# A decoder layer with Strassen-like products: sixteen modulations of single token tiles on VectorE instead of ScalarE, and one store of FF1 on ScalarE's queue

## The chip, the cores and the metric

One core of a Trainium2 chip. It has five engines that each work through a list of their own: TensorE (PE, with its weight loads as PEld), VectorE (DVE), ScalarE (ACT), GpSimd (POOL) and SyncE (SP), and 16 DMA engines that several queues share. The queues are named for the engine that issues to them: in the table of queues of the profile q1 is SP's, q10 is ACT's and q0 is POOL's. The time is the device time of one execution in microseconds, as the median of several runs of the same program.

## The reference

One layer of a decoder trunk, 1024 tokens by 1024 channels, in float32. The part around the change:

```python
x  = layer_norm(ALPHA * x + (1.0 + gt1) * mixed, ln1_g, ln1_b)
u2 = x * (1.0 + sc2) + sh2
h  = square(relu(u2 @ w_ff1 + b_ff1))              # 1024 -> 4096
x  = layer_norm(ALPHA * x + (1.0 + gt2) * (h @ w_ff2 + b_ff2), ln2_g, ln2_b)
```

`mixed` comes from attention and a gated delta rule, whose work lies before the change. `sc2` and `sh2` have one value for each channel; the kernel folds the gain and shift of the first norm into them.

## The kernel before

All large products are made from two-part numbers: a float32 tile is split into a high part (ACT copies it into the rounded format, line 215) and a low part (DVE subtracts, line 216), and each product takes three matmuls: high by high, low by high, high by low. Names that end in `h` and `l`, or `wh` and `wl`, are such parts. A matmul of 128x512 takes 0.23 us from start to start.

FF1 and FF2 are further made with seven products in place of eight, so sums and differences of blocks are needed of the tokens, of the weights and of h. The 1024 tokens are eight tiles of 128, and `TILE = [[0, 2, 4, 5], [1, 3, 6, 7]]` puts them into two halves. A pair of tiles, one of each half, has one number j.

**Order.** PE, DVE and ACT run in program order: `at(p, f)` puts a function at position p, `after(n, f)` n positions from now, and `run_events` calls what is due ahead of each matmul. A position is one 128x512 matmul. What an engine is given by an earlier event stands ahead of what a later one gives it, whether its inputs are there or not. The DMAs issued on SP and POOL are ordered by the scheduler, and those on ACT stand in ACT's own list.

**From the mix to FF1.** The stage that ends the mix has four segments of 96 matmuls. As its token tiles are ended, `mix_done` normalises them (lines 1356 to 1368). Then `u2_turn(j, us, ks)` transposes a tile on PE, four blocks of 128x128 to one PSUM bank (line 1379, tile `b`, two banks in turn), and `put` writes each block with scale and shift into `rawu` (line 1382): position 2 + i after the transposes for block i. Tiles 0 to 3 are turned in pairs, two blocks of either half at a time (`n` = 2). Tiles 4 to 7 come one at a time (`n` = 1): two calls for each, of four blocks. Tiles 6 and 7 are turned after FF1 has begun. `rawu` is then split by `quad_split` into `u11`, `u21` and `u22`, and after the sums of `t_sums` and `t_one` by `t_split` into `mh` and `ml`, which FF1 reads from its fifth product on (the matmul that writes `c` from `mh`).

**FF1.** Sixteen pairs of blocks of `w_ff1`, seven products of 12 matmuls each (line 1841). `w_go` and `w_split` split the weights of the next pair, `f_sums` and `f_sums2` (DVE, lines 1407 and 1516) make their sums in `fraw`. Biases, relu and squares are on ACT (lines 1558 to 1578). The block results `t` (six buffers) are stored to `hf_d` (line 1554) in pieces c0, c2 and c3 by ACT's queue, and the sums: `h_sums` (line 1585 on) makes S1 in `a21` and S2, S3 in `sa`, which go out by SP's queue, as `h_sums2` does with `sb`. `again` (line 1581) reads c0 back for the first five pairs.

**FF2.** It reads `hf_d` and weights in 56 chunks `sraw` of two tiles (lines 1706 and 1712), splits them to `sp` and multiplies (line 1901). The first two chunks are loaded on ACT's queue while FF1 still runs, the rest by SP.

Of the kernel before, what the change touches and what calls it, by code (L numbers as in the profile page):

```python
# [12 lines left out]
AF = mybir.ActivationFunctionType  # L13
ALU = mybir.AluOpType
# [3 lines left out]
P = 128  # L18
# [16 lines left out]
def hybrid_layer_kernel(ctx: ExitStack, tc: tile.TileContext,  # L35
                        x, c, w_ada, b_ada, w_in, conv_w, a_log, dt_bias, sinks, dn_norm_w,
                        w_oa, w_ob, w_out, ln1_g, ln1_b, w_ff1, b_ff1, w_ff2, b_ff2,
                        ln2_g, ln2_b, out, dbg=None):
    nc = tc.nc
    x, c, out = x[0], c[0], out[0]  # L40
# [6 lines left out]
    V, A, G, T = nc.vector, nc.scalar, nc.gpsimd, nc.tensor  # L47
# [7 lines left out]
    def psum(tag, bufs, name=None):  # L55
        return ps.tile([P, HALF], F32, tag=tag, bufs=bufs, name=name or tag)
# [140 lines left out]
    def at(p, f, *args):  # L197
        order[0] += 1
        heapq.heappush(events, (p, order[0], f, args))

    def after(n, f, *args):
        at(count[0] + n, f, *args)
# [62 lines left out]
    sh2 = const.tile([P, KT], F32, name="sh2")  # L265
    sc2 = const.tile([P, KT], F32, name="sc2")
# [182 lines left out]
    for step in steps.split():  # L449
        f, k = step[0], int(step[1])  # L450
# [50 lines left out]
    with tc.tile_pool(name="pa", bufs=2, side="right") as pa:  # L501
        if True:
# [43 lines left out]
            for m in (13, 11, 9, 7, 5, 3, 1):  # L546
# [5 lines left out]
                                   op0=ALU.mult, op1=ALU.mult)  # L552
# [69 lines left out]
        for h in range(8):  # L622
# [7 lines left out]
            for half in range(2):  # L630
                tp = psum("c", 1) if half else psum("b", 2)
                for j in range(4):
                    n = 4 * half + j
                    T.transpose(tp[:, j * P:(j + 1) * P], kT[:, n * P:(n + 1) * P], ident)
                for j in range(4):
                    n = 4 * half + j
# [7 lines left out]
                                   op0=ALU.mult, op1=ALU.mult)  # L644
# [3 lines left out]
            for half in range(2):  # L648
                V.tensor_tensor(out=kd[:, halves[half]].rearrange("p (n c) -> p n c", n=4),
                                in0=tps[half].rearrange("p (n c) -> p n c", n=4),  # L650
                                in1=bc(kdc[:, 4 * half:4 * half + 4, h:h + 1], [P, 4, P]), op=ALU.mult)
            (nc.sync if h == 7 else nc.gpsimd).dma_start(out=kd_d[h], in_=kd)
            for half in range(2):
                kk = psum("a", 2)
                for j in range(4):
                    n = 4 * half + j
                    kc = kT[:, n * P:(n + 1) * P]
                    T.matmul(kk[:, j * P:(j + 1) * P], lhsT=kc, rhs=kc, start=True, stop=True)
                for j in range(4):
                    n = 4 * half + j  # L660
                    V.scalar_tensor_tensor(out=mt[:, n, :], in0=kk[:, j * P:(j + 1) * P],
                                           scalar=nbrk2[:, n, h:h + 1], in1=e[:, n * P:(n + 1) * P],
                                           op0=ALU.mult, op1=ALU.mult)
# [662 lines left out]
    U, rawu = {}, {}  # L1326
# [45 lines left out]
    def u2_turn(j, us, ks):  # L1372

        if 0 in us and ks[0] == 0:
            rawu[j] = [big2.tile([P, 4, 2, P], F32, tag=f"{c}{6 + j % 2}", name="rawu") for c in "hl"]
        tp, n = psum("b", 2), len(us)
        for i, k in enumerate(ks):
            for v, u in enumerate(us):
                T.transpose(tp[:, (n * i + v) * P:(n * i + v + 1) * P], rs[TILE[u][j]][:, k * P:(k + 1) * P], ident)

        def put(i, k):
            A.activation(out=rawu[j][k // 4][:, k % 4, us[0]:us[0] + n].rearrange("p u c -> p (u c)"),
                         in_=tp[:, n * i * P:n * (i + 1) * P],
                         func=AF.Identity, scale=sc2[:, k:k + 1], bias=sh2[:, k:k + 1])
        for i, k in enumerate(ks):
            after(2 + i, put, i, k)

# [18 lines left out]
    def sub(E, out, a, b):  # L1406
        E.tensor_tensor(out=out, in0=a, in1=b, op=ALU.subtract)
# [107 lines left out]
    def add_(E, out, a, b):  # L1515
        E.tensor_tensor(out=out, in0=a, in1=b, op=ALU.add)
# [36 lines left out]
    def put(m, i, t, q=None):  # L1553
        (q or nc.sync).dma_start(out=hf_d[m - 1, i], in_=t)
# [30 lines left out]
    def h_sums(i):  # L1585

        a11, a21, a22 = tls[i, 0], tls[i, 1], tls[i, 3]
        sa = sums_[i] = big2.tile([P, 2, HALF], F32, tag="h7", name="sa")
        sub(V, sa[:, 1], a11, a21)
        add_(V, a21, a21, a22)  # L1590
        sub(V, sa[:, 0], a21, a11)
        put(5, i, a21)
        nc.sync.dma_start(out=hf_d[5:7, i].rearrange("m p c -> p m c"), in_=sa)

    def half_s(j):
# [52 lines left out]
    for i in range(NPAIR):  # L1648
        e = max(pos[i, 3], pos[i, 7]) + 12
        if i < EARLY:  # L1650
            at(e - 24, again, i)
        at(e + 24, h_sums, i)
        at(pos[i, 4] + 32, h_sums2, i)
# [22 lines left out]
    for n in range(NPAIR):  # L1676
        p = pos[n, 1] - 8 if n > EARLY else F0 + 100 + 68 * n
# [122 lines left out]
    for s in range(7 * NS):  # L1800
        p = G0 + 24 * s
# [178 lines left out]
```

## Time and profile before

| | us |
|---|---|
| three runs | 1854.19, 1856.39, 1857.03 |
| median | 1856.39 |
| the profiled execution | 1855.65 |
| its span | 1853.9 |
| PE busy | 1819.3 (98%) |
| DVE busy | 1280.6 (69%) |
| ACT busy | 1023.1 (55%) |
| POOL busy | 318.3 (17%) |
| TensorE clock granted | 0.993 |
| FF1 begins, FF2 begins (PE) | 1223.64, 1542.57 |

How to read it: a timeline row has the start from the beginning of the span, the length, the engine, the line, the operation, the names out<-in and, in brackets, how long the engine was idle ahead of it and what ended that. Rows of several equal instructions in a row carry their count and the length from first start to last end. "ACTq" and "SPq" are issues of DMAs. A group of instructions has the count, busy time and mean ns, then the idle time ahead of the group and what ended it. Matmuls overlap, so a row of 0.39 us is followed by the next 0.23 us later. A list of waits has the waiter, what it waited for, us in total, times, and the longest.

### The profile page before, as it was taken

How to read it: one execution, taken by the hardware profiler on the slowest of the kernel's cores; microseconds unless marked ns; L12 is line 12 of the kernel's file. 1: busy time of each engine (PE TensorE's matmuls, PEld its weight loads, DVE VectorE, ACT ScalarE, POOL GpSimd, SP SyncE). 2: the span in 40 equal slices, each digit the busy share in tenths (PEclk: the TensorE clock that was granted, in tenths of full speed). 3: DMA queues.
4: the chain of work that ended last, by engine and by line, in shares of the span. 5: the costliest groups of instructions: out<-in, count | busy, mean ns of one | idle time of the engine just before them, and what ended most of it. 6: DMA issues, size and time to landing. Idle time of an engine off the chain costs nothing.

```text
span 1853.9 us, 26172 instructions
## 1 busy us (share of the span) xinstructions
PE 1819.3 (98%) x9161; PEld 1504.5 (81%) x9161; DVE 1280.6 (69%) x2411; ACT 1023.1 (55%) x2297; POOL 318.3 (17%) x465
## 2 busy tenths in 40 slices
PE   8999999999999999999999999999999999999997
PEld 6877878888888888888878888877788887888886
DVE  5677688888865666666554445788867676576697
ACT  4689668888874454554454332465555555434341
POOL 0223334454331000000001110002212120000000
PEclk8999999999999999999999999999999999999999
DMA  9645642232258454454345644359887869755671
GB/s 278 185 163 198 215 104 79 85 99 72 71 190 229 139 148 132 147 149 142 109 161 203 193 150 149 123 170 306 314 276 263 269 247 395 271 183 182 198 256 46
DMA packets 262670, 337.74 MB, mean 182 GB/s; under 512 B 26261, under 2 KB 171366, under 8 KB 262282
## 3 DMA queue, kind: packets, MB, share of 16 engines
q1 hardware_dynamic: 223210, 212.94, 36.6%
q0 software_dynamic: 31328, 108.44, 17.3%
q10 hardware_dynamic: 8000, 14.68, 2.2%
q8 instruction: 72, 1.18, 0.3%
q14 instruction: 60, 0.49, 0.1%
HBM read 231.40 MB, written 102.51 MB: 180 GB/s over the span
## 4 chain that ended last, share of the span: by engine, by line
PE 81%; DVE 5%; ACT 4%; DMA 4%; issue 2%; POOL 1%; SPq 0%; ACTq 0%; POOLq 0%; DVEq 0%
PE mm L248 35%; PE mm L1841 7%; PE mm L1901 6%; PE b L1901 4%; PE a L1901 4%; PE b L1841 3%; PE a L1841 2%; PE mm L1470 2%; PE c L1901 2%; PE c L879 1%; PE a L1470 1%; PE mm L188 1%; PE mm L187 1%; PE mm L186 1%; DMA sraw<-in_w_ff_dram 1%
## 5 line engine op out<-in xcount | busy, mean ns | idle before, releaser
L248 PE MATMUL mm<-uh,wl 128*128 128x512 f32 x800 | 331.3, 414 | 0.0
L248 PE MATMUL mm<-ul,wh 128*128 128x512 f32 x800 | 320.7, 401 | 0.0
L248 PE MATMUL mm<-uh,wh 128*128 128x512 f32 x800 | 317.2, 397 | 0.0
L216 DVE TENSOR_TENSOR sp<-sraw,sp 128x1024 fp32r<-128x1024 f32 x112 | 132.8, 1220 | 77.3 <-ACT sp L215 77.2
L215 ACT ACTIVATE sp<-sraw 128x1024 fp32r<-128x1024 f32 x112 | 112.7, 1054 | 122.9 <-PE b L1901 75.4
L248 PEld LDWEIGHTS mm<-ul,wh 128*128 128x128 f32 x800 | 150.6, 188 | 26.6 <-issue 0.2
L248 PEld LDWEIGHTS mm<-uh,wl 128*128 128x128 f32 x800 | 151.3, 189 | 22.8 <-issue 4.0
L248 PEld LDWEIGHTS mm<-uh,wh 128*128 128x128 f32 x800 | 151.6, 189 | 21.2 <-issue 0.2
L1901 PE MATMUL mm<-sp 128*128 128x512 f32 x528 | 137.0, 390 | 1.0 <-DVE sp L216 1.0
L1901 PEld LDWEIGHTS mm<-sp 128*128 128x128 f32 x528 | 98.5, 188 | 22.0 <-DVE sp L216 1.7
L216 DVE TENSOR_TENSOR wl<-wr,wh 128x1024 fp32r<-128x1024 f32 x81 | 100.0, 1234 | 8.8 <-ACT wh L215 8.8
L215 ACT ACTIVATE wh<-wr 128x1024 fp32r<-128x1024 f32 x81 | 85.1, 1051 | 21.3 <-PE c L1470 13.9
L1901 PE MATMUL a<-sp 128*128 128x512 f32 x336 | 92.6, 389 | 0.0
L1140 ACT ACTIVATE vn<-a,brk 128x128 f32<-128x128 f32 x64 | 23.5, 368 | 108.3 <-PE a L1138 107.3
L1901 PE MATMUL b<-sp 128*128 128x512 f32 (+1 forms) x336 | 80.0, 374 | 0.0
L812 DVE CUSTOM_DVE_ANT_0 nscore<-a,amask,nsink 128x256 f32<-128x256 f32 (+1 forms) x128 | 54.6, 464 | 35.5 <-PE a L805 34.7
L864 POOL TENSOR_SCALAR_AFFINE_SELECT pl<-ph 128x512 fp32r<-128x512 f32 x56 | 64.8, 1157 | 74.6 <-DVE ph L857 61.4
L1901 PEld LDWEIGHTS a<-sp 128*128 128x128 f32 x336 | 63.1, 188 | 13.1
L1901 PEld LDWEIGHTS b<-sp 128*128 128x128 f32 x336 | 60.5, 188 | 11.2
L216 DVE TENSOR_TENSOR wl<-fraw,wh 128x1024 fp32r<-128x1024 f32 x43 | 52.6, 1223 | 20.8 <-ACT wh L215 20.4
L823 POOL TENSOR_TENSOR sm<-sm 128x256 f32<-128x256 f32 x56 | 50.2, 897 | 94.0 <-ACT sm L819 51.8
L819 ACT ACTIVATE sm<-nscore,stat 128x257 f32<-128x257 f32 (+1 forms) x128 | 61.9, 486 | 3.3 <-DVE stat L812 3.0
(522 smaller groups left out, 4661.4 us busy)
## 6 DMA issues: line engine op xcount, KB each, us to landing
wr<-in_w_in_dram SPq DMA_DIRECT2D x60, 512.0 KB, 3.6
sraw<-hf_d SPq DMA_DIRECT2D x54, 512.0 KB, 4.5
adaw<-in_w_ada_dram SPq DMA_DIRECT2D x73, 256.0 KB, 4.6
fraw<-in_w_ff_dram SPq DMA_DIRECT2D x32, 512.0 KB, 5.4
sraw<-wt_d SPq DMA_DIRECT2D x32, 512.0 KB, 4.3
hf_d<-t ACTq DMA_DIRECT2D x48, 256.0 KB, 4.3
wt_d<-wx POOLq DMA_DIRECT2D x48, 256.0 KB, 3.0
sraw<-in_w_ff_dram SPq DMA_DIRECT2D x22, 512.0 KB, 5.6
```

What stands on the lines that cost most here:

```text
L186: T.matmul(t, lhsT=wh[:, k, :], rhs=xh[k][:, sl], start=k == 0, stop=False)
L215: A.activation(out=hi, in_=src, func=AF.Copy)
L216: after(lag, lambda: V.tensor_tensor(out=lo, in0=src, in1=hi.bitcast(F32), op=ALU.subtract))
L248: T.matmul(ts[half], lhsT=w[:, k, :], rhs=xx[k][:, sl], start=k == 0 and m == 0, stop=k == KT - 1 and m == 2)
L812: V.tensor_tensor_reduce(out=ns[:, i, 1:1 + W], in0=sc[:, i * 2 * P:i * 2 * P + W], in1=amask[:, mo:mo + W], scale=-1.0, scalar=nsink[:, 2 ...
L819: A.activation(out=sm[:, i, 0:1 + W], in_=ns[:, i, 0:1 + W], func=AF.Exp, scale=-1.0, bias=st[:, i:i + 1], accum_out=st[:, 2 + i:3 + i])
L823: G.tensor_tensor(out=sm[:, :, 1 + P:1 + 2 * P], in0=sm[:, :, 1:1 + P], in1=sm[:, :, 1 + P:1 + 2 * P], op=ALU.add)
L864: G.affine_select(out=flat4(part), in_=flat4(full), pattern=[[0, 4], [1 if odd else -1, P]], compare_op=ALU.is_ge if odd else ALU.is_gt, f ...
L1140: after(1, lambda: A.activation(out=vn, in_=Wp[:, 0:P], func=AF.Copy, scale=brk[:, n, h:h + 1]))
L1470: T.matmul(pt, lhsT=m[k][:, tok], rhs=w[:, k % 2, :], start=k == 0 and w is wh and m is mh, stop=k == KT - 1 and m is ml)
L1841: T.matmul(pt, lhsT=a[:, k0 + k, :], rhs=b[k], start=begin and k == 0 and x_ == 0, stop=k == 3 and x_ == 2, skip_group_check=True)
L1901: T.matmul(to, lhsT=a[:, f, t * P:(t + 1) * P], rhs=b[:, f, lo:up], start=(begin or own) and s % NS == 0 and f == 0 and x_ == 0, stop=s % ...
```

## The change

`put` writes a block on DVE if the tile is turned alone and the block's number is odd: of 32 such puts 16 move, 8 for tiles 4 and 5 ahead of FF1's start and near it, 8 for tiles 6 and 7. In `h_sums`, the store of S1 is put on ACT's queue ten positions after the sums, 16 times; before it was handed to SP's queue at once.

```diff
         def put(i, k):
-            A.activation(out=rawu[j][k // 4][:, k % 4, us[0]:us[0] + n].rearrange("p u c -> p (u c)"),
-                         in_=tp[:, n * i * P:n * (i + 1) * P],
-                         func=AF.Identity, scale=sc2[:, k:k + 1], bias=sh2[:, k:k + 1])
+            dst = rawu[j][k // 4][:, k % 4, us[0]:us[0] + n].rearrange("p u c -> p (u c)")
+            src = tp[:, n * i * P:n * (i + 1) * P]
+            if n == 1 and k % 2:
+                V.tensor_scalar(out=dst, in0=src, scalar1=sc2[:, k:k + 1], scalar2=sh2[:, k:k + 1], op0=ALU.mult, op1=ALU.add)
+            else:
+                A.activation(out=dst, in_=src, func=AF.Identity, scale=sc2[:, k:k + 1], bias=sh2[:, k:k + 1])
         for i, k in enumerate(ks):
             after(2 + i, put, i, k)
...
         sub(V, sa[:, 0], a21, a11)
-        put(5, i, a21)
+        after(10, put, 5, i, a21, A)
```

In the lists below, lines behind the edit in `put` are three higher than in the profile of before: 1410 and 1519 there are 1407 and 1516. The puts of before are line 1382; now they are line 1385 on DVE and 1387 on ACT. A name in brackets is the counter that an instruction waits for.

DVE's list from the statistics of the last mix tiles to the start of FF1, with the puts of tiles 4 and 5:

```order
 L1362 BN_AGGR st<-parts 128x2 [waits DVE_49]
-L216 TENSOR_TENSOR wl<-wr,wh 128x1024 [waits DMAHW2_49,Activation_49]
-L216 TENSOR_TENSOR u11l<-rawu,u11h 128x2x128 [waits Activation_49] x2
-L216 TENSOR_TENSOR u21l<-rawu,u21h 128x2x128 [waits Activation_49] x2
-L216 TENSOR_TENSOR u11l<-rawu,u11h 128x2x128 [waits Activation_49] x2
+L1385 TENSOR_SCALAR rawu<-b,sc_119,sh_118 128x128 [waits Activation_49] x2
+L216 TENSOR_TENSOR wl<-wr,wh 128x1024 [waits DMAHW2_49]
+L1385 TENSOR_SCALAR rawu<-b,sc_119,sh_118 128x128 [waits Activation_49] x4
+L216 TENSOR_TENSOR u11l<-rawu,u11h 128x2x128 [waits DVE_49] x2
+L1385 TENSOR_SCALAR rawu<-b,sc_119,sh_118 128x128 [waits Activation_49] x2
+L216 TENSOR_TENSOR u21l<-rawu,u21h 128x2x128 [waits DVE_49] x2
```

Eight puts have come in, each with a wait for ACT, and the four `u11l` and the two `u21l` stand behind them; the two `u11l` of tile 5 come last, behind the rows shown. On ACT's list the puts that are left, except the first of each bank, wait for DVE.

DVE's list in the first pair of FF1, with the sums of `fraw` and the puts of tiles 6 and 7; two puts stand ahead of these rows, on either side of a weight split:

```order
 L1410 TENSOR_TENSOR x<-fraw 128x512 [waits DMAHW6_49,DMAHW4_49]
 L1519 TENSOR_TENSOR fraw<-fraw 128x512 [waits DMASW4_49,DVE_49]
 L1410 TENSOR_TENSOR fraw<-fraw 128x512 [waits DMASW3_49,DVE_49]
 L1410 TENSOR_TENSOR fraw<-fraw 128x512 [waits DVE_49]
-L1410 TENSOR_TENSOR rawu<-rawu 128x4x128 [waits Activation_49]
-L216 TENSOR_TENSOR u22l<-rawu,u22h 128x2x128 [waits Activation_49] x2
+L1385 TENSOR_SCALAR rawu<-b,sc_119,sh_118 128x128 [waits Activation_49] x3
+L1410 TENSOR_TENSOR rawu<-rawu 128x4x128
+L1385 TENSOR_SCALAR rawu<-b,sc_119,sh_118 128x128 [waits Activation_49] x2
+L216 TENSOR_TENSOR u22l<-rawu,u22h 128x2x128 [waits DVE_49] x2
 L216 TENSOR_TENSOR wl<-wr,wh 128x1024 [waits DMAHW7_49]
+L1385 TENSOR_SCALAR rawu<-b,sc_119,sh_118 128x128 [waits Activation_49]
```

Five of the eight puts of tiles 6 and 7 stand between the sums of `fraw` and the split of `u22`, and one behind the weight split.

ACT's list where FF1 ends and the first chunks of FF2 are loaded:

```order
 L1561 ACTIVATE t<-mm,cols 128x512 [waits DMAHW4_49,PE_49]
 L1709 DMA sraw<-hf_d 128x2x512
-L1715 DMA sraw<-in_w_ff_dram 128x2x512 [waits DMAHW6_49]
-L1709 DMA sraw<-hf_d 128x2x512 [waits DMAHW0_49,PE_49]
+L1715 DMA sraw<-in_w_ff_dram 128x2x512 [waits DMAHW5_49]
+L1557 DMA hf_d<-t 128x512 [waits DMAHW7_49,DVE_49]
+L1709 DMA sraw<-hf_d 128x2x512 [waits DMAHW1_49,PE_49]
 L1715 DMA sraw<-in_w_ff_dram 128x2x512 [waits DMAHW2_49]
```

The store of S1 of the fifteenth pair has come between the loads of the first and of the second chunk. In FF1 the sixteen stores stand on ACT's list in the same way, each right behind the store of c2 of the pair.

## The prediction

> **What bounds the kernel now.** I read the page first, then who the matmul engine waits for around the changed lines, then windows and engine timelines there.
>
> ```profile
> span 1853.9 us, 26172 instructions
> PE 81%; DVE 5%; ACT 4%; DMA 4%; issue 2%; POOL 1%; SPq 0%; ACTq 0%; POOLq 0%; DVEq 0%
> ```
>
> The profiled execution took 1855.65 us, 1.75 more than its span and 0.74 under the median of 1856.39; sums below start from 1855.65. The chain that ended last is 81% PE, so an edit elsewhere counts only where it opens or closes a gap of PE. Waits of PE between 1150 and 1300 us:
>
> ```profile
> PE mm L1841 <- ACT t L1558: 1.8, 1, 1.8
> PE b L1379 <- ACT rawu L1382: 1.6, 3, 1.0
> PE c L1841 <- DVE wl L216: 0.5, 1, 0.5
> PE c L1841 <- ACT wh L215: 0.2, 1, 0.2
> ```
>
> Four microseconds in all, 1.6 of it for the line that is changed (columns: total, times, longest). So relieving ACT can win little there. What it can lose depends on DVE:
>
> ```profile
> 1215.00:1228.00 13.00, 11.55 (x57) 8.84 (x56) 8.80 (x20) 11.65 (x29) 1.81 (x3) 1.00 0.65 207
> 1228.00:1241.00 13.00, 12.97 (x66) 10.43 (x65) 12.29 (x20) 10.27 (x27) 0.53 (x1) 1.00 0.82 253
> 1241.00:1255.00 14.00, 13.35 (x58) 10.43 (x56) 11.99 (x27) 11.91 (x27) 1.63 (x3) 1.00 0.36 114
> ```
>
> These windows (length, then busy PE, weight loads, DVE, ACT, POOL; clock; DMA share; GB/s) cover the single-tile turns. From 1228 on DVE is the fuller engine, 12.29 of 13 us, and it receives the work.
>
> **Edit 1: sixteen puts on DVE.** Prices first.
>
> ```profile
> L593 DVE TENSOR_SCALAR e<-a,r 128x128 f32<-128x128 f32 x64 | 18.2, 343 | 0.0
> L1165 DVE COPY o<-c 128x128 f32<-128x128 f32 x64 | 18.5, 289 | 34.3 <-ACT junk L1164 34.2
> L1382 ACT ACTIVATE rawu<-b,sh,sc 128x128 f32<-128x128 f32 x32 | 12.1, 478 | 1.4 <-PE b L1379 1.0 <-ACT t L1567 0.4
> ```
>
> The first row is the same instruction, shape and source kind (a PSUM tile `a`): 0.34 us, my value. The copy, 0.29, is the low bound; 0.42 (one `u11l` below, 0.76 for two that start 0.34 apart; twice the elements) the high one. An ACT put lasts 0.44 to 0.48. Four of them in a row overlap:
>
> ```profile
> 1217.14 1.49 ACT L1382 ACTIVATE rawu<-b,sh,sc 128x128 f32<-128x128 f32 x4
> 1219.12 2.92 ACT L1382 ACTIVATE rawu<-b,sh,sc 128x128 f32<-128x128 f32 x8
> 1232.29 2.56 ACT L1382 ACTIVATE rawu<-b,sh,sc 128x128 f32<-128x128 f32 x7 [0.62 <-PE b L1379]
> 1238.95 1.51 ACT L1382 ACTIVATE rawu<-b,sh,sc 128x128 f32<-128x128 f32 x4 [0.43 <-ACT t L1567]
> 1252.70 2.01 ACT L215 ACTIVATE wh<-fraw 128x1024 fp32r<-128x1024 f32 x2 [0.40 <-ACT t L1567]
> ```
>
> Four cost 1.49, a start every 0.35. In the changed order each put of a bank waits for the other engine's put before it. The bank is handed ACT, DVE, ACT, DVE; nothing overlaps: 0.46+0.34+0.46+0.34 plus three hand-overs of about 0.04 is 1.72. The hand-over is an estimate from PE's start at 1218.68 below, 0.05 after the last put ended (1217.14+1.49). So even with both engines idle, a bank takes 0.2 longer. The Trainium skill, "PSUM — Partial Sum Buffer", section "PSUM bank collisions raise a hardware error", says to guard PSUM by bank and partition quadrant, not by address; two readers on one bank count as a collision. By that page the serial 1.72 is the price, without it two engines in parallel would give about 0.9; no trace of before has a bank with two readers, the order's waits side with the page.
>
> Now the path of PE, with DVE's queue.
>
> ```profile
> 1218.68 0.66 PE L1379 MATMUL b<-ident,r 128*128 128x128 f32 x4 [0.32 <-ACT rawu L1382]
> ...
> 1221.74 0.66 PE L1379 MATMUL b<-ident,r 128*128 128x128 f32 x4 [1.01 <-ACT rawu L1382]
> ...
> 1223.87 0.40 PE L1841 MATMUL mm<-u11l,wh 128*128 128x512 f32 x1
> ...
> 1226.38 0.39 PE L1841 MATMUL a<-u21h,wh 128*128 128x512 f32 x1
> 1226.89 0.50 PE L1841 MATMUL a<-u21l,wh 128*128 128x512 f32 x1
> ...
> 1234.62 0.60 PE L1379 MATMUL b<-ident,r 128*128 128x128 f32 x4
> ...
> 1253.81 0.50 PE L1841 MATMUL c<-mh,wh 128*128 128x512 f32 x1 [0.19 <-ACT wh L215]
> ```
>
> ```profile
> 1218.22 1.18 DVE L216 TENSOR_TENSOR wl<-wr,wh 128x1024 fp32r<-128x1024 f32 x1
> 1222.38 0.76 DVE L216 TENSOR_TENSOR u21l<-rawu,u21h 128x256 fp32r<-128x256 f32 x2 [2.31 <-ACT u21h L215]
> 1223.06 0.76 DVE L216 TENSOR_TENSOR u11l<-rawu,u11h 128x256 fp32r<-128x256 f32 x2
> ...
> 1233.14 0.69 DVE L1407 TENSOR_TENSOR x<-fraw 128x512 f32<-128x512 f32 x1
> 1234.58 1.42 DVE L1407 TENSOR_TENSOR fraw<-fraw 128x512 f32<-128x512 f32 x2
> 1237.07 0.76 DVE L216 TENSOR_TENSOR u22l<-rawu,u22h 128x256 fp32r<-128x256 f32 x2 [0.46 <-ACT u22h L215]
> 1246.29 1.22 DVE L216 TENSOR_TENSOR wl<-wr,wh 128x1024 fp32r<-128x1024 f32 x1
> 1253.79 1.23 DVE L216 TENSOR_TENSOR wl<-fraw,wh 128x1024 fp32r<-128x1024 f32 x1 [1.97 <-ACT wh L215]
> ```
>
> *Tile 4, first bank.* DVE is busy with statistics until 1218.22. Then DVE 0.34, ACT 0.46, DVE 0.34 and hand-overs: free at 1219.45 where PE now goes on at 1218.68, +0.8. *Next bank.* Its alternation ends near 1221.7, when PE is released today; the 1.01 gap pays the 0.8 back. Net 0.
>
> *Start of FF1.* Today the second matmul takes `u11l` at 1223.87, which DVE began at 1223.06. Tile 5's last bank is transposed as before, by 1222.4, and alternates from 1222.8 (ACT first ends its splits, a little sooner than today) for the 1.72 above, to about 1224.55. Only then come two `u21l` and the first `u11l`: two starts 0.34 apart, then 0.42, done by 1225.54 (the first u21l starts at 1224.48, as an instruction's end overlaps the next start by some 0.08). PE starts this matmul at 1225.58: +1.7. The gap today before the first use of `u21l` (1226.38+0.39 to 1226.89, 0.12) goes, so **+1.6**. DVE's idle 2.31 at 1222.38 absorbs the other puts.
>
> *Tiles 6 and 7.* The put of piece 5 of tile 6 stands behind the four 0.7 us sums of `fraw` (1233.14 to 1234.58+1.42=1236.00), which two earlier puts delay by 2 x 0.34, a little is absorbed: it runs 1236.69 to 1237.03. ACT's piece 6 follows to 1237.54, DVE's piece 7 to 1237.92. Only then is the bank free for tile 7's second transposes: 1237.96 against 1234.62, **+3.4 in all** for PE. ACT stands meanwhile before piece 6 until 1237.07, where today it has seven puts done by 1232.29+2.56=1234.85.
>
> *The tail on DVE.* What ACT does between, a bias, a weight split, `u22h`, a squaring and a store, begins 3.9 later; less the 0.43 that it idles today, its first put of the last bank (1238.95) comes at 1242.42, +3.5. DVE has done piece 1 of tile 7, a sum over `rawu` (0.68) and piece 3 by 1239.16 and waits for that put until 1242.92: 3.8 us idle in an engine that had none to give. And the order puts that wait ahead of the `u22l` splits, which today run at 1237.07. They now start at 1243.19, **+6.1**. Behind them stand a weight split, three sums over `rawu`, the `ml` splits and the `wl` of 1246.29, in a queue busy 11.99 of 14 us whose one real hole, 1.97, is just ahead of 1253.79, the row where it waits for ACT. ACT's `mh` splits need DVE's sums, and its `wh` at 1252.70 stands behind them. PE takes that `wh` at 1253.81. All three therefore come about 6.1 later. PE is released at 1259.95. Its waits on the way (1.6, then 3.4) are part of the 6.1, not added to it. With 0.28 for the DVE put the same walk gives +5.0, with 0.40 and shorter transfers +7.25; if one hole more is found, +4.2. After 1260 FF1 has hardly any gaps of PE in which to win it back; I count **+6.1**.
>
> **Edit 2: the store of S1.** Sixteen issues leave SP's queue and enter ACT's, ten matmuls later.
>
> ```profile
> 1285.47 0.69 DVE L1516 TENSOR_TENSOR t<-t 128x512 f32<-128x512 f32 x1
> ```
>
> ```profile
> 1286.25 0.33 ACTq L1554 DMA_DIRECT2D hf_d<-t  x1
> 1291.34 0.69 ACT L1558 ACTIVATE t<-mm,cols 128x512 f32<-128x512 f32 x1 [5.12 <-DMA hf_d<-t]
> ```
>
> The sum S1 is ready at 1286.16. Ten positions later, ACT has just issued another store (1286.25, 0.33 long), so this one follows at about 1286.6 with nothing to wait for. Its 16 x 0.33 = 5.3 us of issue falls into ACT's idle time, here the 5.12 that it waits next. That wait itself, the 1.8 of PE in the first list, is for a store that ACT issued earlier:
>
> ```profile
> 1284.05 7.18 DMA hf_d<-t
> ```
>
> Moving S1 does not shorten it by anything certain: S1 is on another ring than before but moves the same 256 KB at the same time. I take 0, and keep −1.8 (all of that wait gone) as an end. On SP, `again` loads and later the `rr` loads move up one or two places; none has a waiter near.
>
> One place is different, the start of FF2. The order shows S1 of pair 14 on ACT's queue between the loads of the first two FF2 chunks.
>
> ```profile
> 1524.00:1541.00 17.00, 17.00 (x77) 14.08 (x76) 7.79 (x10) 6.79 (x10) 3.81 (x8) 1.00 1.03 399
> ```
>
> ```profile
> q10 hardware_dynamic: 1251, 2.39, 37.5%
> ```
>
> ```profile
> 1523.62 17.26 DMA sraw<-in_w_ff_dram
> ```
>
> ```profile
> PE mm L1901 <- DVE sp L216: 1.0, 2, 0.8
> ```
>
> All DMA engines are full (share 1.03, 399 GB/s); ACT's ring, q10, moved 2.39 MB in 17 us, and the load issued at 1523.62 takes 17.26 us and lies on the chain; PE waits 0.8 for what it feeds. So 0.26 MB ahead of it in its ring count one to one. By the total rate they cost 0.26/399 GB/s = 0.66 us, by this ring's share 0.26 MB x 17/2.39 = 1.85, and 2.4 if its slowest stretch sets it. SP's ring gets shorter by as much, which speaks for the lower part: **+1.0**. The Trainium skill, "DMA: Bandwidth & Descriptors", section "Queues, rings and completion order", says that a DMA engine goes round between the queue rows that have work, packet by packet. By that page ACT's ring keeps its share whatever SP's holds, and the term would be 1.85; the profile's near-equal shares (37.5% here) agree but cannot show it.
>
> **Sum:** 1855.65 + 6.1 + 1.0 = 1862.75; the median stood 0.74 above that execution, 1863.5. I say 1863.0.
>
> **Rivals.**
> *ACT was the limit and is relieved.* Sixteen puts at 0.35 are 5.6 us off ACT. If DVE takes each at once, PE's gaps of 0.32, 1.01, 0.12, 0.19 and 0.5 close: 2.1 us, 1853.5, with a lost 1.0 at FF2 1854.5. It decides if puts find DVE idle when their bank is ready. For it: DVE 8.80 of 13 busy until 1228. Against: 12.29 of 13 after, and the splits behind the puts.
> *The backlog is absorbed.* PE pays the two direct stalls, 1.6 or 3.4, and the DVE queue catches up by 1253: 1.6 to 3.4 plus 0 to 1.0, 1857.3 to 1860.1. For it: the 1.97 hole. Against: it lies behind the work that is late.
> *The store costs more.* ACT's queue goes in order; if a store on it waits for an earlier transfer (stores took 7 us at 1284), splits behind it slip, in one or two pairs by 1 or 2 us, and FF2 pays 2.4: 1865 to 1868.
> *The change is not what it says.* The order shows 16 puts on DVE and 16 stores on ACT, no more and no less; I give this nothing.
>
> **How the numbers follow.** Chances: forecast (1860.1 to 1865) 0.60; absorbed 0.18; ACT relieved, including −1.8 at the c3 store, 0.12; store dearer 0.10. Range 1857.0 to 1867.5: from the low end of "absorbed" to most of "dearer". About 0.2%, 3.7 us, is what a measurement of this kernel tells from no change, so "slower" begins at 1860.1: forecast and dearer, 0.70, with a little of "absorbed" with its store term, 0.73. "Same", 1852.7 to 1860.1: most of "absorbed" and of "relieved", 0.22. Faster: both "relieved" and the 1.8 together, 0.05.
>
> **What would show it.** Right: PE idle near 1.7 before the second `u11l` matmul of FF1, waiting for DVE; near 1.8 before tile 7's second transposes, now for a DVE put; a wait on ACT's puts for DVE's near 3 us; DVE idle 3 to 4 us ahead of the put behind ACT's; `c<-mh,wh` of the first pair about 6 later; the `sraw` load on ACT's queue at FF2 landing a microsecond later. Wrong: no wait of ACT's puts for DVE's (banks shared freely), `u11l` on time, or PE's later gaps, the 1.8 above all, shrinking by as much as the first ones grew.

## The result and the profile after

| | before | after |
|---|---|---|
| runs of this comparison | 1854.19 to 1859.38, median 1857.03 | 1863.41 to 1870.95, median 1868.25 |
| ratio | | 1.0052, 95% interval 1.0036 to 1.0067 |
| a second comparison, same kernel | median 1859.36 | 1867.36, ratio 1.0054 (1.0036 to 1.0071) |
| profiled execution, its span | 1855.65, 1853.9 | 1868.25, 1866.2 |

The change makes the kernel slower, by 0.5%: 1.0052 of 1857.03 is 9.7 us more, with an interval of 6.7 to 12.4. The ratio is taken over all the runs of a comparison and is not the quotient of the two medians; that quotient is 1.0060 the first time and 1.0043 the second. Forecast were 6.6 us (1863.0 against the median of 1856.39) to 7.1 (the sum). The median of 1868.25 lies 0.75 above the upper end of the forecast's range, 1867.5; the ratio applied to the earlier median of 1856.39 gives 1866.0, which lies in it.

The spans differ by 12.3, but not all of that is the change's. In the profile after, tile 4's first transposes, which stand ahead of every changed instruction, begin at 1220.86 instead of 1215.93: 4.9 us of the difference are older. In the profile before:

```profile
1215.93 0.60 PE L1379 MATMUL b<-ident,r 128*128 128x128 f32 x4
```

The chain of work that ended last in the profile after shows where most of them come from (3.8 us, between 580 and 590), some 640 us earlier, in the stage of the delta rule:

```profile
572.50 15.24 DMA adaw<-in_w_ada_dram
```

That load of weights took 15.24 us; in the profile before the same load took 12.31. The lead (the difference at tile 4's first transposes) changes from execution to execution: it lies between 0.0 and 5.9 us in the thirteen profiled here after the first. So below, **PE's position is counted from tile 4's first transposes**; what is left of the 12.3 is 7.4.

Who PE waits for between 1150 and 1300 us, in the profile after (the waits of before are in the prediction; lines are three higher now, and `u11l` is a row that was not there):

```profile
PE b L1379 <- DVE rawu L1385: 3.6, 3, 2.0
PE b L1844 <- DVE wl L216: 2.1, 1, 2.1
PE mm L1844 <- DVE u11l L216: 1.6, 1, 1.6
PE c L1844 <- ACT wh L215: 1.0, 1, 1.0
PE c L1844 <- DVE wl L216: 0.5, 1, 0.5
PE b L1379 <- ACT rawu L1387: 0.3, 1, 0.3
```

Four microseconds of waits have become more than nine, and DVE is the engine named. The wait of 1.8 for ACT's `t`, the longest before, is not in this list because it comes at 1303 now; it is 0.96 there. PE's timeline gives the places:

```profile
1220.86 0.60 PE L1379 MATMUL b<-ident,r 128*128 128x128 f32 x4
...
1224.59 0.66 PE L1379 MATMUL b<-ident,r 128*128 128x128 f32 x4 [1.29 <-DVE rawu L1385]
1226.98 0.66 PE L1379 MATMUL b<-ident,r 128*128 128x128 f32 x4 [0.34 <-DVE rawu L1385]
1230.85 0.50 PE L1844 MATMUL mm<-u11l,wh 128*128 128x512 f32 x1 [1.59 <-DVE u11l L216]
1243.51 0.66 PE L1379 MATMUL b<-ident,r 128*128 128x128 f32 x4 [1.99 <-DVE rawu L1385]
1259.66 0.50 PE L1844 MATMUL b<-u11h,wl 128*128 128x512 f32 x1 [2.09 <-DVE wl L216]
1265.90 0.50 PE L1844 MATMUL c<-mh,wh 128*128 128x512 f32 x1 [0.96 <-ACT wh L215]
```

From such rows and those of before: the first `u11l` matmul 1230.85 - 1223.87 - 4.93 = +2.05, tile 7's second transposes 1243.51 - 1234.62 - 4.93 = +3.96, the first matmul on `mh` 1265.90 - 1253.81 - 4.93 = +7.16. DVE's timeline shows what it does instead of working:

```profile
1224.13 0.41 DVE L1385 TENSOR_SCALAR rawu<-b,sc,sh 128x128 f32<-128x128 f32 x1 [0.53 <-ACT rawu L1387]
...
1242.11 0.40 DVE L1385 TENSOR_SCALAR rawu<-b,sc,sh 128x128 f32<-128x128 f32 x1
1243.04 0.76 DVE L1385 TENSOR_SCALAR rawu<-b,sc,sh 128x128 f32<-128x128 f32 x2 [0.53 <-ACT rawu L1387]
...
1248.53 0.41 DVE L1385 TENSOR_SCALAR rawu<-b,sc,sh 128x128 f32<-128x128 f32 x1 [3.79 <-ACT rawu L1387]
1248.86 0.75 DVE L216 TENSOR_TENSOR u22l<-rawu,u22h 128x256 fp32r<-128x256 f32 x2
```

And ACT, meanwhile:

```profile
1238.69 0.46 ACT L1387 ACTIVATE rawu<-b,sh,sc 128x128 f32<-128x128 f32 x1 [0.23 <-PE b L1379]
1242.55 0.81 ACT L1387 ACTIVATE rawu<-b,sh,sc 128x128 f32<-128x128 f32 x2 [3.40 <-DVE rawu L1385]
1243.84 0.46 ACT L1387 ACTIVATE rawu<-b,sh,sc 128x128 f32<-128x128 f32 x1 [0.48 <-DVE rawu L1385]
...
1248.04 0.46 ACT L1387 ACTIVATE rawu<-b,sh,sc 128x128 f32<-128x128 f32 x1 [0.43 <-ACT t L1570]
1248.98 0.46 ACT L1387 ACTIVATE rawu<-b,sh,sc 128x128 f32<-128x128 f32 x1 [0.48 <-DVE rawu L1385]
```

The two engines wait for each other in turn. The puts of one bank share a tile `rawu` too, but the trace speaks for the bank: ACT's split `u11h` at 1223.99 reads `rawu` for 0.40 us, and DVE's put of 1224.13 writes another block of the same `rawu` tile in that time. ACT stands 3.40 us for a DVE put that is behind the sums of `fraw`, and 0.48 for an ordinary one; then DVE stands 3.79 us for an ACT put that is behind ACT's other work, with the `u22` splits queued behind it. The list of who waits for the sixteen DVE puts (us, times) sums this up:

```profile
  ACT rawu L1387: 6.9, 7
  PEld b L1379: 5.3, 4
  PE b L1379: 3.6, 3
```

### The profile page after: what moved, and what is told of

Its sections match the earlier page's. It is cut to its first block, busy times and chain, and to the rows that moved or that the text cites. A ratio compares the mean times of both kernels' runs of the same rounds, so it can differ in the third digit from the quotient of the medians.

```text
span 1866.2 us, 26158 instructions
## 1 busy us (share of the span) xinstructions
PE 1820.5 (98%) x9161; PEld 1504.3 (81%) x9161; DVE 1286.0 (69%) x2427; ACT 1018.8 (55%) x2281; POOL 317.1 (17%) x465
## 4 chain that ended last, share of the span: by engine, by line
PE 77%; DVE 8%; DMA 5%; ACT 4%; issue 2%; POOL 0%; ACTq 0%; SPq 0%; DVEq 0%; POOLq 0%
PE mm L248 33%; PE mm L1844 7%; PE mm L1904 6%; PE b L1904 4%; PE a L1904 4%; PE b L1844 3%; PE a L1844 2%; PE c L1904 2%; PE c L879 1%; PE mm L1473 1%; PE mm L188 1%; DMA adaw<-in_w_ada_dram 1%; PE mm L187 1%; PE mm L186 1%; DMA sraw<-in_w_ff_dram 1%
```

## The experiments

Each kernel below computes what the first one does. For each, one execution's PE position, as above, against that of the kernel before, in us. The columns are the first `u11l` matmul (1223.87 before), tile 7's second transposes (1234.62), the first matmul on `mh` (1253.81), the last matmuls of FF1 and the end; the last column is the ratio of whole times with its interval. A ratio has about 3 us of uncertainty either way and one position at the end about 1, since the wait near 1290 changes between executions (0.6 to 2.1 us by the lists of waits, whatever the kernel). In the kernel before, FF1's last matmul begins at 1536.39 and FF2's first at 1536.62 (the table of the profile before has 1542.57, which is wrong).

| kernel | `u11l` | tile 7 | `mh` | FF1's end | end | ratio |
|---|---|---|---|---|---|---|
| changed kernel | 2.0 | 4.0 | 7.2 | 6.8 | 7.4 | 1.0052 (1.0036, 1.0067) |
| the same again | 2.0 | 3.9 | 7.1 | 6.3 | 9.8 | 1.0054 (1.0036, 1.0071) |
| modulations only | 2.2 | 4.1 | 7.7 | 7.4 | 7.0 | 1.0027 (1.0011, 1.0044) |
| store only | 0.0 | 0.0 | 0.0 | -0.2 | 0.5 | 1.0005 (0.9988, 1.0022) |
| last two blocks of a bank | 1.4 | 2.8 | 3.1 | 2.9 | 2.8 | 1.0012 (0.9998, 1.0027) |
| whole second banks | -0.1 | 1.2 | 0.9 | 1.1 | 0.6 | 1.0008 (0.9993, 1.0023) |
| tiles 4 and 5 only | 2.0 | 1.4 | 1.4 | 2.1 | 1.8 | 1.0014 (1.0002, 1.0026) |
| tiles 6 and 7 only | 0.0 | 3.3 | 6.5 | 6.7 | 6.4 | 1.0027 (1.0010, 1.0043) |
| without the last two puts | 2.1 | 4.0 | 4.2 | 3.7 | 3.5 | 1.0028 (1.0013, 1.0043) |
| one bank of tile 5 | -1.0 | -1.4 | -1.3 | -1.8 | -1.4 | 0.9991 (0.9974, 1.0008) |
| sums of `fraw` later | 2.1 | 1.9 | 9.0 | 8.1 | 7.8 | 1.0054 (1.0032, 1.0076) |
| store without the 15th pair | 0.0 | 0.0 | 0.0 | -0.7 | -0.6 | 1.0010 (0.9997, 1.0024) |
| change without that store | 2.3 | 4.2 | 7.4 | 7.7 | 7.5 | 1.0039 (1.0025, 1.0054) |

**The two edits apart.** First the modulations alone:

```diff
-        after(10, put, 5, i, a21, A)
+        put(5, i, a21)
```

> Only the modulations on DVE, the store of S1 as before. PE's position against the kernel before, counted from the last matmul ahead of the change (before 1218): theory (the bank is handed to and fro, and DVE's list carries the wait on): +7.4 after the first matmul that writes c from mh, as in the changed kernel (12.09 - 4.73), of it +1.2 at tile 4, +1.7 at the first u11l matmul, +2.2 at tile 7's second bank, the rest by 1254. At the end near +7. Rival (the store of S1 costs a good part): +4 or less at the end. In all +0.4% of the time.

+7.7 at `mh`, +7.0 at the end; the steps are those of the changed kernel. The loss in FF1 is the modulations'. Part of the 7.7 is the clock: at the wait of 2.1 us for `wl` the granted clock of this execution fell to 0.50 for 3.4 us from 1260.2 on, where in the profile after it stayed at 1.00. The last section comes back to this.

Then the store alone, with `put` of before:

```diff
-        put(5, i, a21)
+        after(10, put, 5, i, a21, A)
```

> Only the store of S1 on ACT's queue. Theory: no step before 1285; the wait of 1.8 us near 1290 as it is or up to 0.8 shorter, +0.6 to +1.0 at the start of FF2, -0.5 to +1.0 at the end. Rival (stores on ACT's list hold up splits): +2.4 or more, with several new waits of PE for ACT between 1290 and 1520.

Nothing up to `mh`, -0.2 at FF1's end, +0.5 at the end. One wait of PE for ACT inside FF1 is new, 0.48 us for `t` at 1283.1 (the matmul of 1276.5 before). The kernel with whole second banks below, whose stores are those of before, has 0.89 at the same matmul, so the store is not needed for it, and the wait near 1290 is 1.2 shorter here.

**How often a bank changes hands.** The same sixteen puts on DVE, as the last two of each bank:

```diff
-            if n == 1 and k % 2:
+            if n == 1 and k % 4 > 1:
```

> Modulations only, and again 16 of 32 on DVE, but of each bank the last two blocks, so that a bank is handed over once and not three times. Theory (the hand-overs make the loss): about +2 at the end, +1.2 at the first u11l matmul, the largest step at tile 7's second bank. Rival (DVE is full, 16 more instructions on it cost what they cost, wherever they stand): +5 to +7, as with every second block.

+2.8: nearer to the +2 than to the +5 of the rival, with the same work on DVE. And sixteen puts that share no bank with ACT:

```diff
-            if n == 1 and k % 2:
+            if n == 1 and k > 3:
```

> Modulations only, again 16 of 32 on DVE, but the whole second bank of each tile, so that no bank is read by two engines. Theory: the gap of 1.0 at 1221.7 goes, about +1.5 comes at tile 7's second bank, which waits for DVE behind the sums of fraw, 0 to +0.5 at the end. Rival (DVE is full): +5 to +7.

+0.6 at the end. The gap at 1221.7 goes (-1.1), but PE waits 0.84 for `u11l` soon after, and the step at tile 7 is there (-0.7 at its first transposes, +1.2 at its second). So with three hand-overs of a bank the sixteen puts cost 7.0, with one 2.8, with none 0.6, by one trace each; the whole times, 5.0, 2.2 and 1.5 us by their ratios, have the same order, but their intervals overlap. A full DVE accounts for little of it; who waits for whom on a shared bank, for most. The number of hand-overs alone is not isolated by this: the three kernels also put their blocks at different places of the two lists.

**Where in the program.**

```diff
-            if n == 1 and k % 2:
+            if n == 1 and k % 2 and TILE[us[0]][j] < 6:
```

> Modulations only, and of them only the eight of tiles 4 and 5 on DVE. PE's position against before, from just ahead of 1218. Theory: +1.2 at tile 4, back to +0.5 at the next bank, +1.7 at the first u11l matmul, +1.6 by 1231, then the gaps of 0.19 and 0.53 near 1254 pay some of it back: +0.6 to +1.2 at the end. Rival (a late DVE never catches up): +1.6 or more stays.

+1.4 at `mh` and +1.8 at the end. The rival is nearer: the gaps of 0.2 and 0.5 near 1254 stayed in PE's list of waits and paid nothing back. What ends them, ACT's and DVE's weight splits, may itself have come later; no run tests that alone.

```diff
-            if n == 1 and k % 2:
+            if n == 1 and k % 2 and TILE[us[0]][j] > 5:
```

> Modulations only, and of them only the eight of tiles 6 and 7 on DVE. Theory: nothing before 1230, about +1 at tile 7's first bank, +3.2 at its second, +5.4 to +6.5 after 1254 and at the end, so that both parts together give about what every second block gives (+7). Rival (DVE catches up, since nothing is late when FF1 begins): +3.4 or less at the end.

+3.3, +6.5 and +6.4. The two parts give 1.8 and 6.4, against 7.0 together.

```diff
-            if n == 1 and k % 2:
+            if n == 1 and k % 2 and not (TILE[us[0]][j] == 7 and k > 3):
```

> Modulations only, as in the changed kernel but with the last two DVE puts, blocks 5 and 7 of tile 7, back on ACT (14 on DVE). Theory (DVE's wait of 3.8 us for ACT ahead of the u22 splits makes the last 3.4 us of the loss): as before up to +4.0 at tile 7's second bank, then no more, +3.0 to +3.5 at the end; DVE's 3.8 us wait is gone. Rival (the later part is only the same lateness carried on, plus 0.36 a put): +6 at the end.

+4.0 at tile 7's second bank and +4.2 at `mh`, where the changed kernel has 7.2. Two puts less, 0.8 us of work, take 3 us away in the trace. The whole times do not show it (1.0028 against 1.0027 with all sixteen, each with some 3 us of uncertainty). DVE's timeline of this kernel has a 1.42 us wait where the changed kernel has 3.79 and a put:

```profile
1240.35 0.41 DVE L1385 TENSOR_SCALAR rawu<-b,sc,sh 128x128 f32<-128x128 f32 x1
1242.18 0.76 DVE L216 TENSOR_TENSOR u22l<-rawu,u22h 128x256 fp32r<-128x256 f32 x2 [1.42 <-ACT u22h L215]
```

**The sums that the prediction blamed for tile 7's wait.**

```diff
-    at(F0 + 32, f_sums, 0, V)
-    at(F0 + 33, f_sums2, 0, V)
+    at(F0 + 56, f_sums, 0, V)
+    at(F0 + 57, f_sums2, 0, V)
```

> Modulations only, but the four sums over fraw of the first pair 24 positions (5.4 us) later, so that no put of tiles 6 and 7 stands behind them. Rival as the prediction has it (the puts wait behind the sums, and what comes later follows from that): the step of 2.2 at tile 7's second bank goes, and 3 to 4 at the end. Theory after the runs so far (the hand-overs on the last bank, behind ACT's own work, make the loss after it on their own): the step goes, but PE is +6 again by 1254, +5.5 to +7 at the end.

The step at tile 7 goes (1.9 instead of 4.1), so the sums are what that put stood behind. But PE waits twice as long a little later. DVE still waits 3.79 us for ACT, and the sums, moved to 1254.5, now stand among the `ml` splits ahead of a `wl`, for which PE waits:

```profile
1259.79 0.80 PE L1844 MATMUL b<-u11h,wl 128*128 128x512 f32 x1 [4.22 <-DVE wl L216]
```

At this matmul PE is +6.3, as in the changed kernel (+6.3) and as the theory has it. The +9.0 at `mh` is something else. After the wait the granted clock (the last but two of these columns, which are those of the windows in the prediction) was 0.50:

```profile
1260.00:1266.00 6.00, 6.00 (x15) 4.70 (x16) 4.86 (x13) 3.85 (x7) 1.09 (x2) 0.50 0.52 162
```

The matmuls start 0.43 us apart there instead of 0.23, and PE goes from +6.3 to +9.3; soon after `mh` it is +8.0. So the theory held as far as the wait for `wl`: what was won at tile 7 was lost again there, since this `wl` begins as late as in the changed kernel (+7.2 in both). What the wait at tile 7 is worth alone is not settled: the sums took 2.8 us of DVE wherever they stood.

**A whole bank where DVE is idle.** Only the first bank of tile 5, all four blocks of it, on DVE:

```diff
-            if n == 1 and k % 2:
+            if n == 1 and TILE[us[0]][j] == 5 and k < 4:
```

> Only the four blocks of the first bank of tile 5 on DVE, all others on ACT: no bank is shared, and DVE idles there (2.3 us before 1222.4). Theory: the gap of 1.0 at 1221.7 goes, -1.0 there, -1.0 to -1.4 at the end. Rival (any put on DVE delays its splits): 0 to +1 at the end.

DVE takes the four at once in its idle time (four rows in one, 1.36 us) and the wait at 1221.7 is gone from PE's list:

```profile
1220.44 1.36 DVE L1385 TENSOR_SCALAR rawu<-b,sc,sh 128x128 f32<-128x128 f32 x4
1221.71 0.76 DVE L216 TENSOR_TENSOR u11l<-rawu,u11h 128x256 fp32r<-128x256 f32 x2
```

-1.4 at the end. It is the only version that is ahead of the first kernel from the changed lines on (the -0.6 of the store without the 15th pair comes from the wait near 1290), but 0.1% cannot be told from no change by the whole times (0.9991, interval 0.9974 to 1.0008).

**The store, and the rest of the whole time.** The changed kernel a second time:

> The changed kernel once more, for its whole time beside the kernel before. The trace of its first execution puts +7.4 us behind the change (12.3 at the end less 4.9 that it was late before the change began); the first comparison gave 1.0052, some +9.7. If the trace is all there is: a ratio of 1.0040. If the change costs something that the trace's stretch does not show: 1.0050 or more again.

The ratio is 1.0054, and this execution's trace accounts for all of it: lead 0.0, +7.1 at `mh`, +6.3 at FF1's end, +9.8 at the end. The 3.4 more come in the first 15 us of FF2. The chain of this second execution names the load on ACT's queue:

```profile
1529.98 19.59 DMA sraw<-in_w_ff_dram
```

and PE's timeline the wait:

```profile
1550.76 0.49 PE L1904 MATMUL mm<-sp 128*128 128x512 f32 x1 [2.18 <-ACT sp L215]
```

The wait explains 2.3 of the 3.4. After it and the next, of 0.76, the granted clock was 0.50 for 3.4 us from 1552.7 on, and the matmuls took longer to start (five in 1.75 us here, in 1.26 in the profile after):

```profile
1552.02 1.96 PE L1904 MATMUL mm<-sp 128*128 128x512 f32 x5 [0.76 <-DVE sp L216]
```

That is another 1.6; a later gap gives 0.5 back. Then the store alone, but for the fifteenth pair:

```diff
-        after(10, put, 5, i, a21, A)
+        after(10, put, 5, i, a21, A) if i != NPAIR - 2 else put(5, i, a21)
```

> Only the store of S1 on ACT's queue, but that of the fifteenth pair, which falls between the first loads of FF2, left on SP's. If the +0.65 at FF2's start with all sixteen is that store on ACT's ring: about 0 there (-0.2 to +0.2). If it is scatter of the loads: +0.4 to +1.0 again or a loss elsewhere.

From FF1's end to the end: +0.1 (-0.75 to -0.64 unrounded), where the store of all sixteen gives +0.7. The rest of its -0.6 came at 1290 and is within that wait's scatter. And with the modulations, as the last run:

> The changed kernel, but the store of S1 of the fifteenth pair left on SP's queue. Theory (that one store between the first loads of FF2 costs 0.6 to 3.4, the other fifteen nothing): +7 at FF1's end of stretch as before, no step at FF2's start (-0.5 to +0.2), the load of the second chunk's weights on ACT's queue lands in 16.5 to 17.3 us again, +6 to +7 at the end, a ratio near 1.0035. Rival (stores on ACT's queue cost elsewhere, or the store is not the cause): +8 or more at the end, a ratio of 1.0050 as with all sixteen.

+7.5 at the end, all of it there by `mh`; nothing at FF2's start (7.7 to 7.5). That is half a microsecond over the +6 to +7 expected and under the rival's +8. The ratio is 1.0039, 7.3 us; its interval does not exclude 1.0050. The load in question, by the chain of each kernel, first in the changed kernel, then with the fifteenth store on SP, then with modulations only:

```profile
1535.32 17.87 DMA sraw<-in_w_ff_dram
```

```profile
1534.63 17.00 DMA sraw<-in_w_ff_dram
```

```profile
1536.44 16.84 DMA sraw<-in_w_ff_dram
```

17.0 and 16.8 without the store ahead of it (17.26 before), 17.9 and 19.6 with it. All fourteen traces agree: from FF2's first matmul to ACT's split of that load it is 3.8 to 4.7 us in the eleven executions without the store there, and 5.0, 5.0 and 6.7 in the three with it; from FF1's end to the end PE moves by -0.5 to +0.4 without it and by +0.6, +0.7 and +3.4 with it. That store is the cost, 0.6 to 3.4 us, and the other fifteen cost nothing that shows. Of the difference between 0.6 and 3.4, about 1.1 is the clock after the longer wait, less the gap that is won back; why the load itself took 1.7 us longer in one execution than in the other stays open.

## Why the prediction was right, and where its sizes were off

The direction, the mechanism and its places were right. PE is idle where it was said to be, with 1.59 for 1.7 and 1.99 for 1.8; ACT's puts wait 3.40 for "near 3", DVE idles 3.79 for 3.8 ahead of the last bank, and the edits apart put the loss in FF1 on the puts. The time came out 2.6 to 2.9 us longer than the sum by the whole times, and 0.3 and 2.7 longer by the two traces. That the first trace's 7.4 is so near the sum's 7.1 is in part luck: the puts cost 1.05 more than was said, the store 0.4 less, and 0.4 was won at the wait near 1290, for which the sum had nothing.

- **What bounds the kernel.** PE, with 4 us of waits near the change, so little to win and more to lose: as read. Of the gaps that a relief of ACT could have closed, the 1.0 at 1221.7 was there to be had, as the single bank of tile 5 shows; the others were not tried alone.
- **Tile 4 and the next bank.** Said +0.8, then 0. By PE's rows: 1224.59 - 1218.68 - 4.93 = +0.98, then 1226.98 - 1221.74 - 4.93 = +0.31.
- **Start of FF1.** Said +1.7 at the `u11l` matmul and +1.6 after the next gap; they are +2.05 and +1.89, with a wait of 1.59 and the 0.31 carried in. Tile 5's last bank took 1.83 from its first put to its last (1227.96 to 1229.79, with no other work between), where the sum had 1.72.
- **Tiles 6 and 7.** Said +3.4, a wait of 1.8; they are +3.96 and 1.99. ACT's wait for DVE was said to be near 3, it is 3.40.
- **The tail.** Said: DVE idle 3.8 ahead of the put behind ACT's, `u22l` and all behind it +6.1. DVE idles 3.79, and `u22l` is 1248.86 - 1237.07 - 4.93 = +6.86. The trace of the kernel without the last two puts bears out that this wait makes the last 3 us.
- **The term that was too small** is the price of a DVE put. I took 0.34, from the same instruction in an earlier stage, and kept 0.42 as the high end. By their row among the groups by line (least, median and most ns) it is 0.41:

```profile
L1385 DVE TENSOR_SCALAR rawu<-b,sc,sh x16: 357/409/410, 1223.2 to 1250.7; 128x128 f32<-128x128 f32 x16
```

A pair of puts on a shared bank repeats every 0.94 (0.46 on ACT, 0.48 until its next starts), against the 0.88 of the sum. The walk with 0.40 and shorter transfers had given +7.25, which is where the trace lies (+7.2). So a put of 0.41 fits what the sum fell short; no run shows it alone. And the row of L593 was not quite the same instruction: it reads one value for each partition (`e<-a,r`, its second operand is a constant), the puts read two (`sc`, `sh`). Whether that makes 0.41 out of 0.34 is not shown by a run.
- **Does a bank take two readers at once?** The Trainium skill, "PSUM — Partial Sum Buffer", section "PSUM bank collisions raise a hardware error", has it guarded by bank. The trace agrees in so far as in the rows shown of shared banks a put begins 0.03 to 0.04 after the other engine's has ended (ACT's of 1242.55 lasts some 0.46, DVE's begins at 1243.04), and the three kernels with three, one and no hand-over show what that is worth here (7.0, 2.8, 0.6). What would happen without the guard was not tried.
- **The store.** The fifteen inside FF1 cost nothing, as said. The one at FF2's start was taken at +1.0, with 0.66 and 2.4 as ends (no row shown gives the 2.4); it measures 0.6 and 3.4. So its high end was too low. One reading of the rings did not hold: ACT's ring is not bound to the share that it had. In the stretch of the changed kernel that answers to 1524 to 1541 before, the table of queues reads

```profile
q10 hardware_dynamic: 1413, 2.68, 41.2%
q0 software_dynamic: 657, 2.29, 33.0%
q1 hardware_dynamic: 1021, 1.97, 29.9%
```

so q10 moved 2.68 MB in 17 us where it moved 2.39, and SP's q1 1.97 for 2.18: the store's 0.26 MB were mostly carried by a larger share. But the share does not tell how late the load comes. In the second execution, 1530.35 to 1547.35, it was as large, and the load took 19.59 us and not 17.87:

```profile
q10 hardware_dynamic: 1401, 2.66, 41.4%
```

The Trainium skill, "DMA: Bandwidth & Descriptors", section "Queues, rings and completion order", has the engines go round the queue rows packet by packet; these shares neither prove nor contradict it, but an equal share cannot be read from it.
- **The rival of the backlog absorbed** fell: from `mh` to FF1's end at most 0.8 is won back (7.2 to 6.8 and 7.1 to 6.3), at the wait near 1290 that scatters by more. So did the hope that the kernel with tiles 4 and 5 only would win its 0.7 near 1254.

Added up, +7.2 and the store's +0.6 or +3.4, less some tenths at 1290, give the two traces' 7.4 and 9.8, and the ratios' 9.7 and 10.0 lie at the upper end of that, within their intervals.

## What to carry to other kernels

When half of an engine's small operations are moved to another engine, look at what they share: on one PSUM bank they came one after the other here, and each waits behind everything that stands ahead of its partner in that engine's list, so two fixed orders are locked together three times a bank. Move whole banks, at a place where the receiving engine has a hole, or leave them. And where a queue feeds the stage that starts next, nothing large should be put between its loads, even if the bytes only change rings: here 256 KB cost 0.6 to 3.4 us.

## What the runs showed that was not expected

Executions differ by up to 5.9 us before the changed part is reached. Six of the fourteen traces are over 4 us late there, and all six fall back by 3.8 to 6.5 us between 560 and 600 us, where PE waits 2.6 to 4.3 us in them: in the profile after behind the load of `adaw` that took 15.24 us, in the kernel with the modulations only for another load:

```profile
PE b L1059 <- DMA T<-t_d: 3.2, 1, 3.2
```

The first profile of the kernel before has no wait of PE in that stretch. It is not the only place: the changed kernel without the fifteenth store waits 0.4 us there and is 3.3 late at tile 4. So a position counted from a matmul near the change says more about this kernel than one whole time.

A wait can also cost more than its length, because the granted clock can fall behind it. Between 150 us and the end of the work, every fall in the fourteen traces goes to 0.50 for 3.4 or 6.8 us and comes at a wait of PE of about 2 us or more; all six waits of 2.6 us or more had one, and four of the 22 between 1.8 and 2.6. Which of those do is not shown. The scatter of whole times goes with the clock too: of 101 executions of the kernel before that stood beside the experiments, the five with a mean granted clock of 0.994 have a median of 1854.0 us, the 35 with 0.992 one of 1858.2 and the twelve with 0.990 one of 1862.7.
